# A two-layer encoder on one core: the second layer's SwiGLU of two prompt blocks in one loop, with gate and up as seven block products

## The chip, the core and the metric

One core of a Trainium2 chip runs the program. TensorE (PE) multiplies, VectorE (DVE), ScalarE (ACT) and GpSimd (POOL) do elementwise work, and DMA queues, issued here nearly always by SyncE (SP), move data between DRAM and on-chip memory. Each engine runs its own instructions in order and waits for the others by semaphores. The metric is the time of one execution in device microseconds (us). The kernel before takes 3156.17 us, the median of three runs (3152.59 to 3156.47).

## The reference

Two layers; the first mixes tokens with a Fourier transform, the second with attention; each is followed by a SwiGLU. Two sequences go through the same weights: a sample of 512 tokens and a prompt of 1024. Width is 1024, the hidden width of the SwiGLU is 2816.

```python
def swiglu_ffn(x, g, w_gate, w_up, w_down):
    h = rms_norm(x, g)
    return (jax.nn.silu(h @ w_gate) * (h @ w_up)) @ w_down

for i in range(DEPTH):
    j = i // 2
    if i % 2 == 0:
        x = x + fourier_mixer(x, norm_mix[i], fourier_w[j])
    else:
        x = x + attention_mixer(x, norm_mix[i], attn_w_qkv[j], attn_q_norm[j],
                                attn_k_norm[j], attn_w_o[j], cos, sin)
    x = x + swiglu_ffn(x, norm_ffn[i], w_gate[i], w_up[i], w_down[i])
```

## The kernel before, in words

Tokens are cut into three blocks of 512: block 0 is the sample, blocks 1 and 2 the prompt. Activations lie transposed, features on the 128 partitions and 512 tokens along them, so a block is 8 tiles of 128x512. Float32 matmuls are made of three: every operand is split into a rounded high half and the low rest (`split`, L219: a copy on ACT, L223, then a subtraction, L224, on POOL for weights and on DVE for the hidden chunk), and `mm3` (L229) multiplies high by high, high by low and low by high (L230 to L232). Its third matmul alone needs the low half of the weight.

`ffn(layer, b, ...)` (L636) is one SwiGLU of one block. It goes over 22 chunks of 128 hidden features. For each it loads three 128x1024 weights (gate, up, down; `weights`, L234, with buffers `raw` and `w`), makes gate and up into the two banks `g` with 24 matmuls each, then Silu on ACT (L675), the product on DVE (L676) and the split into `mid`. The chunk's eight down products (`down`: bank `c`, then an addition into `acc` on DVE, L650) are put on a list, `pend`, and drawn from it one by one between the matmuls of the next chunk.

While `ffn` runs as the main stream, a second stream prepares what comes later; `weave` (L814) mixes the two by paces given in estimated microseconds, and a scheduler then orders the instructions of each engine. The streams have buffers of their own, marked F (main) and X (second): four `w` buffers each, two `raw` each, in PSUM two `g` and two `c` banks for F, a pair of banks `a` and two `c` banks for X. In layer 1 the streams are: block 0's SwiGLU beside `aux_3` (the queries, keys and values of block 2, the attention of blocks 1 and 2, their output projections, `linear_residual` L621, which start from the attention output that `reloaded` L315 reads back from DRAM, and the norm of block 1); block 1's SwiGLU beside the norm of block 2; block 2's SwiGLU alone. The normed input h of a block, high and low, takes one of two buffers `h`. A norm starts with four small matmuls that spread the row factors (`in_rows`, L269), which need the sum of squares that the projection's last piece completes.

## Time and profile before

| what | before |
|---|---|
| median of three runs | 3156.17 us |
| the profiled execution: time, span | 3155.58 us, 3153.8 us |
| granted TensorE clock, mean | 0.989 |
| matmuls | 14646 |
| DMA traffic | 362.38 MB |

The profile gives busy times by engine, windows of the span, waits, and a timeline of single instructions. An entry such as `c<-mid,w` names what an instruction writes and what it reads. Matmuls are pipelined and their ends modelled, so their busy times overlap; the distance between starts is the time that one costs in a stream.

### The profile page before, as it was taken

How to read it: one execution, taken by the hardware profiler on the slowest of the kernel's cores; microseconds unless marked ns; L12 is line 12 of the kernel's file. 1: busy time of each engine (PE TensorE's matmuls, PEld its weight loads, DVE VectorE, ACT ScalarE, POOL GpSimd, SP SyncE). 2: the span in 40 equal slices, each digit the busy share in tenths (PEclk: the TensorE clock that was granted, in tenths of full speed). 3: DMA queues.
4: the chain of work that ended last, by engine and by line, in shares of the span. 5: the costliest groups of instructions: out<-in, count | busy, mean ns of one | idle time of the engine just before them, and what ended most of it. 6: DMA issues, size and time to landing. Idle time of an engine off the chain costs nothing.

```text
span 3153.8 us, 38178 instructions
## 1 busy us (share of the span) xinstructions
PE 3041.1 (96%) x14646; PEld 2523.0 (80%) x14646; DVE 1565.9 (50%) x2812; ACT 1253.2 (40%) x1806; POOL 1272.4 (40%) x583
## 2 busy tenths in 40 slices
PE   5699999999999999999999999999999999999999
PEld 4587788888877778888878788788788888888887
DVE  5664455453465643443464556666235445444444
ACT  5443332333266632333344477777323223222221
POOL 3444744434333454443433321312544444444443
PEclk9799999999999999999999999999999999999999
DMA  4424553333223544433343311212634333333332
GB/s 182 160 77 125 182 165 107 121 96 97 91 90 106 179 151 134 145 102 113 103 139 101 102 58 51 77 44 70 210 130 149 117 98 122 99 127 94 94 101 87
DMA packets 132091, 362.38 MB, mean 115 GB/s; under 512 B 15890, under 2 KB 24082, under 8 KB 131652
## 3 DMA queue, kind: packets, MB, share of 16 engines
q1 hardware_dynamic: 130468, 353.09, 35.3%
q10 hardware_dynamic: 1440, 6.85, 0.5%
q8 instruction: 115, 1.88, 0.2%
q14 instruction: 68, 0.56, 0.1%
HBM read 316.88 MB, written 43.00 MB: 114 GB/s over the span
## 4 chain that ended last, share of the span: by engine, by line
PE 84%; issue 4%; POOL 4%; DVE 3%; DMA 3%; ACT 2%; SPq 0%; POOLq 0%; ACTq 0%; DVEq 0%
PE g L230 14%; PE g L232 14%; PE g L231 14%; PE c L230 11%; PE c L231 11%; PE c L232 11%; POOL w L224 2%; PE c L787 2%; PE a L230 2%; PE a L232 2%; PE a L231 1%; DMA raw<-in_wf_dram 1%; DVE col L770 1%; PE c L720 1%; POOL raw L577 1%
## 5 line engine op out<-in xcount | busy, mean ns | idle before, releaser
L224 POOL TENSOR_TENSOR w<-raw,w 128x1024 fp32r<-128x1024 f32 (+1 forms) x496 | 1170.8, 2373 | 1760.7 <-ACT w L223 1749.9
L650 DVE TENSOR_TENSOR acc<-c,acc 128x512 f32<-128x512 f32 x1056 | 725.7, 689 | 788.1 <-PE c L232 784.1
L230 PE MATMUL g<-h,w 128*128 128x512 f32 x2112 | 830.2, 393 | 6.8 <-DVE h L227 6.5
L232 PE MATMUL g<-h,w 128*128 128x512 f32 x2112 | 826.3, 391 | 0.0
L231 PE MATMUL g<-h,w 128*128 128x512 f32 x2112 | 825.4, 391 | 0.0
L223 ACT CAST w<-raw 128x1024 fp32r<-128x1024 f32 (+1 forms) x496 | 513.8, 1038 | 744.2 <-PE c L232 533.0
L230 PEld LDWEIGHTS g<-h,w 128*128 128x128 f32 x2112 | 397.9, 188 | 86.8 <-DVE h L227 6.8
L232 PEld LDWEIGHTS g<-h,w 128*128 128x128 f32 x2112 | 397.6, 188 | 82.4 <-POOL w L224 0.3
L231 PEld LDWEIGHTS g<-h,w 128*128 128x128 f32 x2112 | 397.8, 188 | 78.9
L230 PE MATMUL c<-mid,w 128*128 128x512 f32 x1056 | 417.4, 396 | 12.2 <-DVE acc L650 9.6
L231 PE MATMUL c<-mid,w 128*128 128x512 f32 x1056 | 414.0, 392 | 0.6 <-DVE mid L224 0.6
L232 PE MATMUL c<-mid,w 128*128 128x512 f32 x1056 | 413.6, 392 | 0.0
L230 PEld LDWEIGHTS c<-mid,w 128*128 128x128 f32 x1056 | 198.7, 188 | 64.4 <-DVE acc L650 21.4
L675 ACT ACTIVATE t<-g 128x512 f32<-128x512 f32 x132 | 78.9, 597 | 404.4 <-PE g L232 404.0
L231 PEld LDWEIGHTS c<-mid,w 128*128 128x128 f32 x1056 | 199.1, 189 | 41.2 <-DVE mid L224 2.0
L232 PEld LDWEIGHTS c<-mid,w 128*128 128x128 f32 x1056 | 199.1, 189 | 41.1
L230 PE MATMUL c<-h,w 128*128 128x512 f32 x480 | 190.0, 396 | 1.4 <-ACT h L223 1.4
L231 PE MATMUL c<-h,w 128*128 128x512 f32 x480 | 188.4, 393 | 0.8 <-POOL h L224 0.8
L232 PE MATMUL c<-h,w 128*128 128x512 f32 x480 | 187.2, 391 | 0.0
L769 DVE TENSOR_REDUCE col<-a 128x1 f32<-128x1024 f32 (+1 forms) x96 | 100.3, 1045 | 127.0 <-PE a L232 126.8
L676 DVE TENSOR_TENSOR g<-g,t 128x512 f32<-128x512 f32 x132 | 92.0, 697 | 142.6 <-PE g L232 139.3
L224 DVE TENSOR_TENSOR mid<-g,mid 128x512 fp32r<-128x512 f32 x132 | 91.0, 690 | 88.1 <-ACT mid L223 87.7
(225 smaller groups left out, 3299.9 us busy)
## 6 DMA issues: line engine op xcount, KB each, us to landing
raw<-in_gate_dram SPq DMA_DIRECT2D x132, 512.0 KB, 3.5
raw<-in_up_dram SPq DMA_DIRECT2D x132, 512.0 KB, 3.6
raw<-in_down_dram SPq DMA_DIRECT2D x132, 512.0 KB, 3.6
t<-xres SPq DMA_DIRECT2D x80, 256.0 KB, 4.2
raw<-in_qkv_dram SPq DMA_DIRECT2D x36, 512.0 KB, 3.5
xres<-t SPq DMA_DIRECT2D x48, 256.0 KB, 3.0
acc<-xres SPq DMA_DIRECT2D x48, 256.0 KB, 4.7
raw<-in_wo_dram SPq DMA_DIRECT2D x24, 512.0 KB, 3.5
```

Of the source, the lines that this page charges most:

```text
L223: act.copy(hi, src)
L224: eng.tensor_tensor(lo, src, hi.bitcast(F32), op=ALU.subtract)
L230: pe.matmul(out, lh, rh, start=first, stop=False)
L231: pe.matmul(out, lh, rl, start=False, stop=False)
L232: pe.matmul(out, ll, rh, start=False, stop=last)
L577: pool.tensor_tensor(f[:, 1], raw[:, 0], raw[:, 1], op=ALU.subtract)
L650: dve.tensor_tensor(acc[dc], ps, acc[dc], op=ALU.add)
L675: act.activation(s, ga, AF.Silu)
L676: dve.tensor_tensor(up, up, s, op=ALU.mult)
L720: pe.matmul(c[:, i : i + 1], sq[:, i * P : (i + 1) * P], ones[:, 0:1], start=True, stop=True)
L769: dve.tensor_reduce(st[:, 0:1], s_in, op=ALU.max, axis=AX.X)
L787: pe.transpose(tr[:, i * P : (i + 1) * P], p[:, kc * P : (kc + 1) * P], ident)
```

## The change

The SwiGLU of blocks 1 and 2 in layer 1 becomes one loop, `ffn_pair`, over eleven pairs of chunks. For a pair, gate (and likewise up) is a product of a weight of 2 x 2 parts (two chunks, two halves of the 1024 features) with an activation of 2 x 2 parts (two halves of the features, two blocks). Instead of eight products of parts it makes seven, after Strassen and Winograd, of sums of parts. Each has one stationary weight operand (`operands`: four raw quarters a11, a12, a21, a22 and POOL's sums of them, each split as before) and one moving operand that is the same for all pairs: B11, B21, T2, T1, B22, T3 and N4, in this order. The results are added on DVE (`plus`) through the buffers U, V and W; with the second, fifth, sixth and seventh product a hidden chunk of one block is complete (`hidden`). Of the products two in three use a pair of banks held as one tile (`a`), every third the two `g` banks.

`moving` makes the seven moving operands from the normed blocks, by groups of four 128x512 pieces; five stay on chip, and T3 and N4 go through one buffer `l` to DRAM (`late`) and come back by a DMA that POOL issues (`moving_late`), into the buffer where block 0's h was. This stage and the first weights are the end of `aux_3`, which is now paced so that all of it ends within block 0's SwiGLU. The second stream's buffers are closed then, and the pair's take their place. The two `h` buffers are now told apart as A and B.

```diff
+    def open_pool(name, **kw):
+        opened[name] = tc.tile_pool(name=name, bufs=1, **kw)
+        pools[name] = opened[name].__enter__()
+        return pools[name]
...
-        "h": 2, "acc": 4, "mid": 2,
+        "hA": 1, "hB": 1, "acc": 4, "mid": 2,
         "wF": 4, "wX": 4, "rawF": 2, "rawX": 2, "tF": 3, "tX": 4, "ssF": 1, "ssX": 2, "pX": 2,
         "gF": 2, "gX": 1, "cF": 2, "cX": 2,
+        "mT": 5, "WT": 1, "tT": 6, "lT": 1, "rT": 4, "gT": 2,
...
+    def moving(blocks, gain, ops):
+        tp = open_pool("tT")
+        yield 2.0
+        r = [in_rows(rstd[b], lambda n: tl("t", [n], F32, "tT", tp)) for b in blocks]
+        yield 1.0
+        for j in range(4):
+            v = {}
+            for k in range(2):
+                for d in range(2):
+                    c = 4 * d + j
+                    x = tl("x", [TB], F32, "tT", tp)
...
+            a2 = bank2()
+            a, b = a2[:, 0], a2[:, 1]
...
+                dve.scalar_tensor_tensor(
+                    a if (d, k) == (0, 1) else x, x, gain[:, 4 * d + j : 4 * d + j + 1], r[k], op0=ALU.mult, op1=ALU.mult
+                )
+            def put(name, src, eng=None):
+                split(ops[name][:, 0, j], ops[name][:, 1, j], src, eng=eng)
+            def put_late(k, src):
+                x = tl("l", [2, TB], F32R, "lT", tp)
+                split(x[:, 0], x[:, 1], src, eng=pool)
+                sp.dma_start(late[:, k, :, j, :], x.bitcast(F32))
+            put("B11", v[0, 0], pool)
+            put("B21", v[1, 0], pool)
+            yield 6.0
+            dve.tensor_tensor(b, a, v[0, 0], op=ALU.subtract)
+            put("T1", b)
+            dve.tensor_tensor(v[0, 1], v[1, 1], a, op=ALU.subtract)
+            put_late(0, v[0, 1])
+            put("B22", v[1, 1], pool)
+            yield 6.0
+            dve.tensor_tensor(b, v[1, 1], b, op=ALU.subtract)
+            put("T2", b)
+            dve.tensor_tensor(v[0, 0], v[1, 0], b, op=ALU.subtract)
+            put_late(1, v[0, 0])
+            yield 6.0
+        close_pool("tT")
...
+    def moving_late(ops, k):
+        if k == 0:
+            m = h_slot("late", F32R, "A")[:, 0 : 16 * TB].rearrange("p (k h c n) -> p k h c n", k=2, h=2, c=4)
+            ops["T3"], ops["N4"] = m[:, 0], m[:, 1]
+        pool.dma_start(ops[("T3", "N4")[k]], late[:, k])
...
+        def some():
+            credit[0] += 0.62
+            while credit[0] >= 1.0:
+                credit[0] -= 1.0
+                if pend:
+                    pend.pop(0)()
...
+        def times(w, x):
+            turn[0] += 1
+            if turn[0] % 3 == 0:
+                banks = [bankg(), bankg()]
+            else:
+                g2 = tl("a", [2, TB], F32, "gT", gt)
+                banks = [g2[:, 0], g2[:, 1]]
+            for i in range(2):
+                for j in range(4):
+                    mm3(banks[i], w[:, 0, 4 * i + j], w[:, 1, 4 * i + j], x[:, 0, j], x[:, 1, j], j == 0, j == 3)
+                    some()
+                yield i, banks[i]
...
+        def operands():
+            for f0 in range(0, NF, 2):
+                a11, a12 = quarter(f0, 0), quarter(f0, 1)
+                yield stationary(a11)
+                a21, a22 = quarter(f0 + 1, 0), quarter(f0 + 1, 1)
+                yield stationary(a12)
+                s1 = raw_tile(2, TB)
+                pool.tensor_tensor(s1, a21, a22, op=ALU.add)
+                pool.tensor_tensor(a21, a11, a21, op=ALU.subtract)
+                pool.tensor_tensor(a11, s1, a11, op=ALU.subtract)
+                yield stationary(a11)
+                pool.tensor_tensor(a12, a12, a11, op=ALU.subtract)
+                yield stationary(s1)
+                yield stationary(a12)
+                yield stationary(a21)
+                yield stationary(a22)
...
+        def step(x):
+            w = ready.pop()
+            ready.append(next(ahead_))
+            yield from times(w, ops[x])
+        U, V, W = (tmp(), tmp()), (tmp(), tl("ss", [TB], F32, "ssF")), tl("W", [TB], F32, "WT", pools["mT"])
+        for f0 in range(0, NF, 2):
+            f1 = f0 + 1
+            for i, ps in step("B11"):
+                act.copy(U[i], ps)
+            if f0 == 0:
+                moving_late(ops, 0)
+                moving_late(ops, 1)
+            wd0 = weights(t["down"][layer, f0])
+            for i, ps in step("B21"):
+                plus(ps, ps, U[i])
+                if i == 0:
+                    s = silu(V[0], ps)
+                else:
+                    hidden(ps, s, f0, blocks[0], wd0)
+            for i, ps in step("T2"):
+                plus(U[i], ps, U[i])
+            for i, ps in step("T1"):
+                plus(V[i], ps, U[i])
+            for i, ps in step("B22"):
+                plus(ps, ps, V[i])
+                if i == 0:
+                    s = silu(W, ps)
+                else:
+                    hidden(ps, s, f0, blocks[1], wd0)
+            wd1 = weights(t["down"][layer, f1])
+            for i, ps in step("T3"):
+                plus(U[i], ps, U[i])
+                plus(ps, ps, V[i])
+                if i == 0:
+                    s = silu(V[0], ps)
+                else:
+                    hidden(ps, s, f1, blocks[1], wd1)
+            for i, ps in step("N4"):
+                plus(ps, ps, U[i])
+                if i == 0:
+                    s = silu(U[0], ps)
+                else:
+                    hidden(ps, s, f1, blocks[0], wd1)
...
+    def paced(stage, f):
+        for v in stage:
+            yield v * f
...
-        yield from qkv(2, kept[2])
-        yield from attend((1, 2))
+        yield from paced(qkv(2, kept[2]), 0.4)
+        yield from paced(attend((1, 2)), 0.65)
         for b in (1, 2):
-            yield from out_projection(b)
-        yield from prepare(1, 1)
-
-    def aux_4():
-        yield 100.0
-        yield from prepare(2, 1)
+            yield from paced(out_projection(b), 0.5)
+        close_pool("ap")
+        close_pool("sbX")
+        tp = open_pool("mT")
+        for name in ("B11", "B21", "T2", "T1", "B22"):
+            ops[name] = tl(name, [2, 4, TB], F32R, "mT", tp)
+        yield from moving((1, 2), g_ffn[1], ops)
+        close_pool("psX")
+        last["pair"] = ffn_pair(1, (1, 2), ops, t["y"])
+        cur[0] = "F"
+        v = next(last["pair"])
+        cur[0] = "X"
+        yield v
...
-    weave(ffn(1, 0, h_next, t["y"][0]), FFN_US, aux_3(), (QKV_US + 240.0 + 2 * LIN_US) * SLACK, 9)
-    weave(ffn(1, 1, h_next, t["y"][1]), FFN_US, aux_4(), 200.0)
-    weave(ffn(1, 2, h_next, t["y"][2]), FFN_US)
+    weave(ffn(1, 0, h_next, t["y"][0]), FFN_US, aux_3(), FFN_US, 9)
+    weave(last["pair"], 1.0)
```

Three places show how the order of instructions changes. First TensorE, where one chunk's last up matmul is followed by the next chunk, before (block 2; `h_21011` is its h):

```order
L231 MATMUL g_22794<-h_21011,w_22785 128x512
L232 MATMUL g_22794<-h_21011,w_22785 128x512
L230 MATMUL g_22904<-h_21011,w_22891 128x512
L231 MATMUL g_22904<-h_21011,w_22891 128x512
L232 MATMUL g_22904<-h_21011,w_22891 128x512
```

and in the changed loop, from the third place after the last matmul of B22's product (`late_19901` holds T3, here with weight `w_20923`, and N4, with `w_20973`; `mid_20965` is the hidden chunk that B22's product completed; in brackets the engines whose semaphores a row waits for):

```order
L244 MATMUL a_20976<-late_19901,w_20923 128x512
L245 MATMUL a_20976<-late_19901,w_20923 128x512
L246 MATMUL a_20976<-late_19901,w_20923 128x512
L244 MATMUL g_21044<-late_19901,w_20973 128x512 [waits Activation_49]
L245 MATMUL g_21044<-late_19901,w_20973 128x512
L244 MATMUL g_21045<-late_19901,w_20973 128x512
L245 MATMUL g_21045<-late_19901,w_20973 128x512
L246 MATMUL g_21044<-late_19901,w_20973 128x512 [waits Pool_49]
L244 MATMUL c_20983<-mid_20965,w_20744 128x512 [waits Activation_49]
```

Before, 18 matmuls of the next chunk's gate (three are shown) stand between the last up matmul and the first that reads `mid`. Now N4's first matmul stands six places after B22's last one, its first use of a low half ten, and the first reader of `mid` eleven.

Second POOL, which before made the low halves of three weights per chunk:

```order
L224 TENSOR_TENSOR w_23567<-raw_23565,w_23567 128x1024 [waits DMAHW5_49,Activation_49]
L224 TENSOR_TENSOR w_23668<-raw_23666,w_23668 128x1024 [waits DMAHW6_49,PE_49,Activation_49]
L224 TENSOR_TENSOR w_23673<-raw_23671,w_23673 128x1024 [waits DMAHW7_49,Activation_49]
L224 TENSOR_TENSOR w_23678<-raw_23676,w_23678 128x1024 [waits DMAHW0_49,Activation_49]
L224 TENSOR_TENSOR w_23779<-raw_23777,w_23779 128x1024 [waits DMAHW1_49,PE_49,Activation_49]
```

and now, from the low half of N4's weight in one pair to that of T2's in the next (`raw_22721`, `raw_22724`, `raw_22787` and `raw_22790` are the next pair's quarters a11 to a22, `raw_22853` their sum):

```order
L238 TENSOR_TENSOR w_22658<-raw_22369,w_22658 128x1024 [waits Activation_49]
L832 TENSOR_TENSOR raw_22853<-raw_22787,raw_22790 128x1024 [waits DMAHW2_49,DMAHW1_49,DMAHW3_49,DMAHW0_49,Pool_49]
L833 TENSOR_TENSOR raw_22787<-raw_22721,raw_22787 128x1024 [waits DMAHW4_49,Pool_49]
L238 TENSOR_TENSOR w_22727<-raw_22721,w_22727 128x1024 [waits Activation_49]
L834 TENSOR_TENSOR raw_22721<-raw_22853,raw_22721 128x1024 [waits Pool_49]
L238 TENSOR_TENSOR w_22793<-raw_22724,w_22793 128x1024 [waits DMAHW7_49,DMAHW6_49,Activation_49]
L836 TENSOR_TENSOR raw_22724<-raw_22724,raw_22721 128x1024 [waits Pool_49]
L238 TENSOR_TENSOR w_22850<-raw_22848,w_22850 128x1024 [waits DMAHW5_49,Activation_49]
L238 TENSOR_TENSOR w_22857<-raw_22721,w_22857 128x1024 [waits PE_49,Activation_49]
```

Between the weights stand four sums, and the first of them waits for the last quarter's load.

Third DVE, with the last chunks of layer 1's block with buffer `acc`; before, one chunk of block 1:

```order
L650 TENSOR_TENSOR acc_19688<-c_21733,acc_19688 128x512 [waits DVE_49,PE_49]
L650 TENSOR_TENSOR acc_19688<-c_21741,acc_19688 128x512 [waits DVE_49,PE_49]
L676 TENSOR_TENSOR g_21666<-g_21666,t_21755 128x512 [waits DVE_49,PE_49,Activation_49]
L224 TENSOR_TENSOR mid_21758<-g_21666,mid_21758 128x512 [waits Activation_49]
L650 TENSOR_TENSOR acc_19687<-c_21796,acc_19687 128x512 [waits DVE_49,PE_49]
L650 TENSOR_TENSOR acc_19687<-c_21804,acc_19687 128x512 [waits DVE_49,PE_49]
```

and now, under the fourth chunk from the end of block 0 (`x_19373` to `x_19377` are pieces of the second group of `moving`, `c_19182` and `c_19195` the row factors):

```order
L744 TENSOR_TENSOR x_19219<-x_19221,a_19227 128x512 [waits Pool_49]
L664 TENSOR_TENSOR acc_12867<-c_19349,acc_12867 128x512 [waits PE_49]
L664 TENSOR_TENSOR acc_12867<-c_19357,acc_12867 128x512 [waits PE_49]
L721 SCALAR_TENSOR_TENSOR x_19373<-x_19373,gains,c_19182 128x512 [waits DMAHW1_49]
L721 SCALAR_TENSOR_TENSOR a_19379<-x_19375,gains,c_19195 128x512 [waits DMAHW6_49,DVE_49]
L690 TENSOR_TENSOR g_19264<-g_19264,t_19388 128x512 [waits PE_49]
L721 SCALAR_TENSOR_TENSOR x_19377<-x_19377,gains,c_19195 128x512 [waits DMAHW7_49,Pool_49]
L238 TENSOR_TENSOR mid_19391<-g_19264,mid_19391 128x512 [waits Activation_49]
```

The chunk's product `g_19264` and its `mid_19391` now stand among the pieces of `moving`, behind one that waits for its load.

More of the change, by code (lines that the diff above doesn't have):

```diff
@@ L213, in trunk_kernel @@
     du = dram.tile([P, 2, 4, 514], F32, name="du")
+    late = dram.tile([P, 2, 2, 4, TB], F32, name="late")
     dot = [dram.tile([P, NC, TB], F32, name=f"dot{b}") for b in range(3)]
@@ L295, in new_residual, with normed @@
             rstd_cols(rstd[b], ss.pop(b), D)
-    def normed(b, gain, got, held=None):
+    def normed(b, gain, got, ab, held=None):
         yield 2.0
         r = in_rows(rstd[b])
-        h = h_tile()
+        h = h_tile(ab)
         yield 1.0
@@ L313, in normed, with reloaded @@
         got["h"] = h
[L315 to L317 removed]
+    def reloaded(d, got, ab):
+        h = h_tile(ab)
         for dc in range(NC):
@@ L344, in stats_rows @@
     def stats_rows(seq, n):
-        s = cp.tile([P, n], F32, name=f"s_{seq}")
-        r = cp.tile([P, n], F32, name=f"r_{seq}")
+        s = mpt.tile([P, n], F32, name=f"s_{seq}")
+        r = mpt.tile([P, n], F32, name=f"r_{seq}")
         xs = whole[seq]
@@ L355, in masked @@
     def masked(r, c):
-        m = cp.tile([P, 2], F32, name=nm("m"))
+        m = mpt.tile([P, 2], F32, name=nm("m"))
         dve.tensor_tensor(m[:, 0:1], r[:, c : c + 1], mask, op=ALU.mult)
@@ L681, in ffn @@
             one()
+    def moving(blocks, gain, ops):
[9 more added lines that the diff above has]
+                    x = tl("x", [TB], F32, "tT", tp)
+                    sp.dma_start(x, xres[blocks[k]][:, c, :])
+                    v[d, k] = x
+            a2 = bank2()
+            a, b = a2[:, 0], a2[:, 1]
+            for (d, k), x in v.items():
+                dve.scalar_tensor_tensor(
[22 more added lines that the diff above has]
+        close_pool("tT")
@@ new lines, in moving_late, with ffn_pair, down, quarter @@
+    def moving_late(ops, k):
[3 more added lines that the diff above has]
+        pool.dma_start(ops[("T3", "N4")[k]], late[:, k])
+    def ffn_pair(layer, blocks, ops, outs):
+        src = (t["gate"], t["up"])
+        raws, gt = open_pool("rT"), open_pool("gT", **PS)
+        accs = {}
+        for b in blocks:
+            halves = [acc_tile("acc", [4, TB], F32) for _ in range(2)]
+            accs[b] = [a[:, i] for a in halves for i in range(4)]
+        credit = [0.0]
+        def down(m, wd, fc, b, dc):
+            ps = bank()
+            mm3(ps, wd[:, 0, dc], wd[:, 1, dc], m[:, 0], m[:, 1], True, True)
+            acc = accs[b][dc]
+            if fc == 0:
+                sp.dma_start(acc, xres[b][:, dc, :])
+            dve.tensor_tensor(acc, ps, acc, op=ALU.add)
+            if fc == NF - 1:
+                new_residual(b, dc, acc, outs[b][:, dc, :])
+        def some():
[4 more added lines that the diff above has]
+                    pend.pop(0)()
+        def quarter(fc, half):
+            raw = tl("raw", [2, TB], F32, "rT", raws)
+            for i in range(2):
+                sp.dma_start(raw[:, i], src[i][layer, fc, :, half * TB : (half + 1) * TB])
+            return raw
+        def stationary(raw):
+            w = w_tile(2, NC, P)
+            flat = w.rearrange("p h c n -> p h (c n)")
+            split(flat[:, 0], flat[:, 1], raw.rearrange("p k n -> p (k n)"), eng=pool)
+            return w
+        turn = [0]
+        def times(w, x):
[5 more added lines that the diff above has]
+                banks = [g2[:, 0], g2[:, 1]]
+            for i in range(2):
+                for j in range(4):
+                    mm3(banks[i], w[:, 0, 4 * i + j], w[:, 1, 4 * i + j], x[:, 0, j], x[:, 1, j], j == 0, j == 3)
+                    some()
+                yield i, banks[i]
+        def hidden(up, s, fc, b, wd):
+            dve.tensor_tensor(up, up, s, op=ALU.mult)
+            m = tl("mid", [2, TB], F32R, "mid")
+            split(m[:, 0], m[:, 1], up)
+            pend.extend(lambda dc=dc: down(m, wd, fc, b, dc) for dc in range(NC))
+        def silu(s, x):
+            act.activation(s, x, AF.Silu)
+            return s
+        def plus(out, ps, x):
+            dve.tensor_tensor(out, ps, x, op=ALU.add)
+        def operands():
[14 more added lines that the diff above has]
+                yield stationary(a22)
+            yield None
+        ahead_ = operands()
+        ready = [next(ahead_)]
+        yield 15.0
+        def step(x):
[41 more added lines that the diff above has]
+                    hidden(ps, s, f1, blocks[0], wd1)
+            yield 1.0
+        while pend:
+            pend.pop(0)()
+        close_pool("gT")
+        close_pool("rT")
@@ L684, in qkv @@
     def qkv(b, held=None):
         got = {}
-        yield from normed(b, g_mix1, got, held)
+        yield from normed(b, g_mix1, got, "BAB"[b], held)
         h = got["h"]
@@ L886, in follow @@
         yield from mixer_projection("s", got_s, ahead)
-        yield from normed(0, g_ffn[0], first)
+        yield from normed(0, g_ffn[0], first, "B")
     def prepare(b, layer):
-        yield from normed(b, g_ffn[layer], nxt)
+        yield from normed(b, g_ffn[layer], nxt, "B" if b == 2 else "A")
     def h_next():
```

66 lines of the change are left out of this document (36 added, 30 removed).

## The prediction

> **What bounds the kernel now.** The page first: which engine is busy, and at what clock.
>
> ```profile
> span 3153.8 us, 38178 instructions
> PE 3041.1 (96%) x14646; PEld 2523.0 (80%) x14646; DVE 1565.9 (50%) x2812; ACT 1253.2 (40%) x1806; POOL 1272.4 (40%) x583
> ...
> PEclk9799999999999999999999999999999999999999
> ```
>
> TensorE (PE) is busy 96% of the span, at full clock after the start; no other engine passes 50%. The order of TensorE's instructions is the same in both programs up to one place: the last matmul of the second chunk of block 1's output projection. The timeline has that place, and windows from it to the end give the rest.
>
> ```profile
> 2229.29 0.39 PE L232 MATMUL c<-h,w 128*128 128x512 f32 x1
> 2229.52 0.39 PE L230 MATMUL g<-h,w 128*128 128x512 f32 x1
> ...
> 2229.50:2421.40 191.90, 191.38 (x853) 157.67 (x852) 80.52 (x145) 60.13 (x84) 83.02 (x40) 1.00 0.46 150
> 2421.40:2781.90 360.50, 360.30 (x1594) 298.23 (x1593) 162.50 (x236) 95.93 (x118) 157.64 (x67) 1.00 0.36 114
> 2781.90:3153.80 371.90, 366.19 (x1610) 301.26 (x1608) 159.09 (x230) 89.32 (x109) 154.54 (x65) 1.00 0.32 101
> ```
>
> The columns after the window are its length, then busy time and count of PE, weight load, VectorE (DVE), ScalarE (ACT) and GpSimd (POOL), then clock. The windows are the rest of layer 1's block 0, then block 1, then block 2. TensorE is full in all three, so what is saved must be matmuls, and what is lost will be waits that are not there today. TensorE's waits from 2400 on:
>
> ```profile
> PE c L230 <- ACT mid L223: 1.5, 1, 1.5
> PE c L230 <- DVE acc L650: 0.3, 1, 0.3
> PE c L231 <- DVE mid L224: 0.2, 1, 0.2
> ```
>
> Two microseconds in 754. The timeline at the end of one chunk of block 2 prices everything that follows:
>
> ```profile
> 2716.52 0.39 PE L232 MATMUL g<-h,w 128*128 128x512 f32 x1
> ...
> 2716.03 4.76 POOL L224 TENSOR_TENSOR w<-raw,w 128x1024 fp32r<-128x1024 f32 x2 [4.60 <-ACT w L223]
> 2716.99 1.06 ACT L223 CAST w<-raw 128x1024 fp32r<-128x1024 f32 x1 [1.03 <-PE g L232]
> 2717.00 0.70 DVE L676 TENSOR_TENSOR g<-g,t 128x512 f32<-128x512 f32 x1 [1.41 <-PE g L232]
> 2717.95 0.58 ACT L223 CAST mid<-g 128x512 fp32r<-128x512 f32 x1
> 2718.46 0.33 SPq L237 DMA_DIRECT2D raw<-in_gate_dram  x1
> 2718.55 0.69 DVE L224 TENSOR_TENSOR mid<-g,mid 128x512 fp32r<-128x512 f32 x1 [0.85 <-ACT mid L223]
> 2720.60 0.39 PE L232 MATMUL g<-h,w 128*128 128x512 f32 x1
> 2720.82 0.39 PE L230 MATMUL c<-mid,w 128*128 128x512 f32 x1
> ```
>
> A matmul lasts 0.39 here, but from 2716.52 to 2720.60 there are 18 steps: 4.08 / 18 = 0.2267 us each. They overlap, and **0.2267 is the price of a matmul**, not 0.39. Others: an engine that waits for a matmul starts 0.47 after its start (2716.99); the hidden chunk has its high half 2.0 us (2718.53) and its low half 2.7 us (2719.24) after the last up matmul. The 18 matmuls put ahead of the first down product, 4.1 us, hide that.
>
> **What is removed.** Today two chunks for two blocks take 4 x 48 = 192 gate and up matmuls; the seven products take 7 x 24 = 168. Over 11 pairs of chunks 264 go: 264 x 0.2267 = **59.8 us**. The down products and the norms' matmuls stay in number. By the mean duration in the groups (393 ns) one would get 104 us, which is wrong, since these matmuls overlap. [...]
>
> **What is added** is work for the other engines, and less distance between producer and consumer.
>
> ```profile
> L224 POOL TENSOR_TENSOR w<-raw,w 128x1024 fp32r<-128x1024 f32 x484 | 1155.6, 2400 | 1739.5 <-ACT w L223 1728.7 <-PE c L232 5.3 <-PE a L232 5.2
> L224 POOL TENSOR_TENSOR h<-t,h 128x512 fp32r<-128x512 f32 x24 | 30.4, 1295 | 7.3 <-ACT h L223 7.3
> L223 ACT CAST w<-raw 128x1024 fp32r<-128x1024 f32 x484 | 506.5, 1048 | 736.7 <-PE c L232 533.0 <-PE g L232 86.9 <-POOL raw L577 47.3
> L650 DVE TENSOR_TENSOR acc<-c,acc 128x512 f32<-128x512 f32 x1056 | 725.7, 689 | 788.1 <-PE c L232 784.1
> L227 DVE SCALAR_TENSOR_TENSOR h<-a,gains,h 128x512 fp32r<-128x512 f32 x64 | 47.8, 748 | 13.2 <-ACT h L226 13.1
> raw<-in_gate_dram SPq DMA_DIRECT2D x132, 512.0 KB, 3.5
> t<-xres SPq DMA_DIRECT2D x80, 256.0 KB, 4.2
> raw<-dqk SPq DMA_DIRECT2D x30, 256.0 KB, 2.7
> ```
>
> A pair is 168 + 96 = 264 matmuls, 59.8 us. In it POOL has 9 low halves of weights and 4 sums of 128x1024, 13 x 2.40 = 31.2 us; DVE has 14 product sums, 8 for the hidden chunks and 32 down additions, 54 x 0.69 = 37.3 us; ACT has 9 x 1.05 + 10 x 0.6 = 15.5 us. **Loads fit; latencies decide.** The sums' price is that of the row of 128x1024, the nearest one.
>
> *Pair loop, weights.* The four weight buffers hold two down chunks, the operand in use and the next one. N4's operand takes the buffer that B22 leaves: 0.47 + 1.05 + 0.08 + 2.40 = 4.0 us after B22's last matmul its low half is there, or 18 matmuls. In the order N4 needs it 10 matmuls after in three of eleven pairs (21 or more in the others): 3 x 8 x 0.2267 = 5.4. Only then is the fourth quarter's raw buffer free: its load (3.4 with the issue, between the 2.7 and 3.5 of the rows), two sums and the low half of the next B11, 3 x 2.40, follow on POOL, 4.0 + 3.4 + 7.3 = 14.7 us or 65 matmuls after B22. The order has B11 at 59, 64, 74, 77, 64, 74, 56, 64, 74 and 59: short by 24 matmuls in all, 5.4.
> *Pair loop, banks.* 52 of the 77 products put gate and up into one tile of two banks, and there the up half waits until the gate half is read. Behind the waiting matmul stands all of TensorE's queue. With a sum alone the reader needs 0.47 + 0.69 + 0.05 = 1.2 us, and the order leaves 4 matmuls between, 1.1 us with the step itself; with Silu too 1.8 against 1.8 (7 matmuls). That is at most 0.1 each, 3 in all, and 36 if a down addition (0.69) always stands ahead on DVE. For the loop I take 5.4 + 5.4 + 3 less what overlaps, **13**; ends 0 and 36.
>
> *The moving operands* are made under the last four chunks of block 0: 288 matmuls, 65.3 us, stand on TensorE behind the norms' rows. In them DVE has 16 x 0.75 + 24 x 0.69 of this stage and 40 x 0.69 of the chunks, 56 us, and POOL 20 x 1.295 + 12 x 2.40, 55 us. Six x buffers serve groups of four, so in groups 2 to 4 a load (4.2) that waits for a buffer stands on DVE ahead of a chunk's g<-g,t, which has 4.1 - 2.7 = 1.4 us to spare: up to 3 x 2.8. I take **6**; ends 0 and 17 (all four groups late by a load).
> *The first pair.* From its start POOL has one weight, two DMA issues, a down weight, four sums and T2's weight, 7 x 2.40 and what is still ahead of them, one more, 19.2 us. T2 wants its low half some 77 matmuls after the start, 17.5 us. A DMA issue from POOL isn't in the trace; SP's is 0.33 us, two make 0.7. I take **3**; ends 0 and 8. [...]
> *Output projections* stand closer together: 60 matmuls lie between the two where 72 did, 2.7 us less cover for reading the attention output back (8 x 1.295 on POOL). I take **2**; ends 0 and 6.
> *End.* Some 15 down products remain after the last N4 in place of 8, and the timeline shows two of them per 1.75 us in place of 1.36:
>
> ```profile
> 3145.72 0.40 PE L230 MATMUL c<-mid,w 128*128 128x512 f32 x1
> ...
> 3147.47 0.40 PE L230 MATMUL c<-mid,w 128*128 128x512 f32 x1
> ```
>
> That is 7 x 0.2 = 1.4 more, and the older ones hide the 1.5 us wait for mid shown above: nothing in all.
> *At nothing:* the two norms of block 1 and 2 (they move from later blocks, where 0.5 us of waits stood), the reload of T3 and N4 through DRAM (needed 156 matmuls, 35 us, after its buffer is free; 2 MB is four times the 3.5 us row), and half the gate and up traffic. Without that cover the reload would cost 14 us once.
>
> **Sum.** 59.8 - 13 - 6 - 3 - 2 = 35.8. The profiled execution took 3155.6 (span 3153.8 and 1.8 around it), the median of the runs is 3156.2: 3155.6 - 35.8 = **3119.8, forecast 3120**.
>
> **Rivals.**
> 1. *TensorE never waits.* All of 59.8 comes: 3096. For it: block 1 and 2 show 0.5 us of waits today, and POOL and DVE are loaded by half. Against it: the order leaves 10 matmuls where 18 are needed. With the terms at half: up to 3108.
> 2. *DVE's or POOL's queue binds in the loop.* The loop's end of 36 in place of 13: 3143; with some of the other ends, up to 3150. For it: 54 DVE instructions per pair in bursts; DVE can be in a down addition when a product ends. Against: DVE is idle 38% of a pair.
> 3. *Slower: weights come late at every product.* A product takes 59.8 / 7 = 8.5 us, and its successor's weight can start only when its predecessor leaves a buffer. With POOL free that takes 4.0 us. Each POOL instruction ahead adds 2.40: with two it is 8.8, with three 11.2. All of the gain is eaten at 59.8 / 77 = 0.8 us per product, so from a little over two ahead at every product. At two and a half ahead, 10.0 - 8.5 = 1.5 x 77 = 116: 3212. Against it: POOL is busy 31 of 60 us, and the order places most operands' first use 30 matmuls or more after the buffer is left.
> 4. *The second stream doesn't end within the first block.* Then TensorE stands at B11. The order has 288 matmuls there; only if the stage took over 125 us would all be lost. Between, some 50 us late: 3165 at the worst; within 0.2% at 30 to 40.
>
> **Chances.** Forecast (3108 to 3132) 0.52; rival 1 0.22; rival 2 0.16; rival 3 0.05; rival 4 0.05. The range leaves out what lies below 3096 (0.03), the far end of rival 2 and the two last: 3096 to 3146. About 0.2% (3150 to 3162) is what a measurement of this kernel can tell from no change. Faster: 0.52 + 0.22 + 0.16 = 0.90; same 0.03 and slower 0.02 of rival 4; with rival 3 slower is 0.07.
>
> **What would show it.** TensorE's count falls by 264 to 14382. In the loop a pair takes 60 to 62 us; waits of PE on POOL's w stand at N4 and at the next B11, and on DVE and ACT at the up halves. Ahead of the loop, DVE waits for x loads, and PE for mid, in the last three chunks of block 0. Wrong would be: pairs of 59.8 (rival 1), of 63 or more (rival 2) or of 68 with POOL without a gap (rival 3), or a PE gap of 10 us before the first product (rival 4).

## The result, and the profile after

The changed kernel takes 3131.7 us, the median of four runs (3126.0 to 3136.2); the kernel before took 3156.2 in the same comparison. The ratio is 0.9924, with a 95% interval of 0.9905 to 0.9943: **24 us faster**, where 36 were forecast (3120, range 3096 to 3146).

The page of after, its lines on the span and the engines:

```profile
span 3134.4 us, 37508 instructions
PE 3005.0 (96%) x14382; PEld 2471.0 (79%) x14382; DVE 1656.4 (53%) x2974; ACT 1243.9 (40%) x1807; POOL 1325.6 (42%) x616
...
PEclk9799999999999999999999999999999999999999
```

TensorE has 264 matmuls less and the same share of busy time. Now windows of after, from the place where TensorE's order begins to differ: attention's rest and output projections, the stage of the moving operands, and from the first product to the end (length, then busy time and count by engine, clock, DMA share, GB/s):

```profile
2233.40:2360.70 127.30, 127.00 (x574) 104.72 (x573) 43.29 (x89) 38.47 (x56) 55.57 (x28) 1.00 0.50 164
2360.70:2434.70 74.00, 68.75 (x290) 54.82 (x289) 51.34 (x80) 31.06 (x47) 49.87 (x32) 0.98 0.58 193
2434.70:3134.40 699.70, 682.89 (x2929) 543.58 (x2927) 399.86 (x604) 166.06 (x209) 342.54 (x145) 1.00 0.20 66
```

They add to 901.0; before, the same work took 191.9 + 360.5 + 371.9 = 924.3. So 23.3 us are gained here. The place itself comes 3.9 us later than before (2233.4 against 2229.5), with the same instructions ahead of it; in the later profiles it comes anywhere from 2224.8 to 2233.4, so this is spread and not the change.

For 2927 steps of 0.2267 the last window would need 663.6 us, and 4.4 go by after the last matmul's start: 31.7 us are stops, that is, time by which the distance of two starts exceeds a step. TensorE's waits in that window name a part of them (engine, line, what it waits for; total, times, longest):

```profile
PE a L246 <- POOL w L238: 6.2, 4, 1.8
PE g L246 <- POOL w L238: 5.1, 6, 1.3
PE c L244 <- DVE acc L771: 0.6, 3, 0.2
PE a L244 <- ACT t L818: 0.2, 1, 0.2
```

L244 to L246 are `mm3` in the changed kernel, L237 and L238 `split`, L771 the pair's down additions, L818 Silu, L822 the additions of products. The third matmul of a weight, which alone needs its low half, waits for POOL. The timeline of the third pair has such a wait at N4's weight:

```profile
2604.76 1.05 ACT L237 CAST w<-raw 128x1024 fp32r<-128x1024 f32 x1 [3.14 <-PE a L246]
...
2605.89 2.38 POOL L238 TENSOR_TENSOR w<-raw,w 128x1024 fp32r<-128x1024 f32 x1 [6.79 <-ACT w L237]
...
2606.66 0.40 PE L245 MATMUL g<-late,w 128*128 128x512 f32 x1
...
2608.29 0.33 SPq L786 DMA_DIRECT2D raw<-in_gate_dram  x1
...
2608.32 0.50 PE L246 MATMUL g<-late,w 128*128 128x512 f32 x1 [1.26 <-POOL w L238]
```

ACT had to wait for B22's last matmul to leave the buffer; the low half was ready at 2608.27, and TensorE, after a last start at 2606.66, went on at 2608.32: 1.43 us more than a step. Only then (2608.29) is the next quarter's load issued.

The view of waits misses the short stops. They can be seen between the starts of neighbouring matmuls, here where B21's up half waits for its tile of two banks (timeline of after):

```profile
2635.32 0.70 DVE L822 TENSOR_TENSOR a<-a,t 128x512 f32<-128x512 f32 x1 [0.74 <-PE a L246]
...
2636.06 0.60 ACT L818 ACTIVATE t<-a 128x512 f32<-128x512 f32 x1 [3.35 <-DVE a L822]
...
2636.41 0.39 PE L244 MATMUL g<-T,w 128*128 128x512 f32 x1
2636.71 0.50 PE L244 MATMUL a<-B,w 128*128 128x512 f32 x1
2637.05 0.40 PE L245 MATMUL a<-B,w 128*128 128x512 f32 x1
2637.28 0.39 PE L246 MATMUL a<-B,w 128*128 128x512 f32 x1
```

The sum and Silu read the gate half until 2636.66. The up half's first matmul starts at 2636.71, 0.30 after its neighbour: a wait of 0.07. But the matmul behind it comes 0.34 later, 0.11 more than a step, and only the next is at 0.23 again. **This stop of 0.07 costs 0.18.**

If each step's excess over 0.2267 is put down to the matmul that waits at its end (the order lists which do), and the excess of the next step to the same stop, each step counted once, the last window divides like this:

| TensorE's stop, from the first product on | stops | waited, us | next steps, us |
|---|---|---|---|
| low half of a product's weight (POOL) | 11 of 77 | 13.1 | 1.1 |
| up half, until its tile's gate half is read (ACT, DVE) | 37 of 52 | 1.6 | 4.0 |
| down product (mid, or its bank `c`; the end too) | 26 | 3.5 | 2.8 |
| first matmul of a product (ACT) | 3 | 0.6 | 0.3 |
| eight steps at half clock (last section) behind one of the late low halves | | | 1.7 |
| steps too long by less than 0.06 | | | 3.0 |

That is 31.7 in all.

### The profile page after: what moved, and what is told of

It is laid out like the page before. It is cut to its first block, busy times and chain, and to the rows that moved or that the text cites. A ratio compares the mean times of both kernels' runs of the same rounds, so it can differ in the third digit from the quotient of the medians.

```text
span 3134.4 us, 37508 instructions
## 1 busy us (share of the span) xinstructions
PE 3005.0 (96%) x14382; PEld 2471.0 (79%) x14382; DVE 1656.4 (53%) x2974; ACT 1243.9 (40%) x1807; POOL 1325.6 (42%) x616
## 5 line engine op out<-in xcount | busy, mean ns | idle before, releaser
L238 POOL TENSOR_TENSOR w<-raw,w 128x1024 fp32r<-128x1024 f32 (+1 forms) x463 | 1093.4, 2371 | 1632.9 <-ACT w L237 1596.3
L237 ACT CAST w<-raw 128x1024 fp32r<-128x1024 f32 (+1 forms) x463 | 479.2, 1038 | 754.8 <-PE c L246 357.2
L244 PE MATMUL g<-h,w 128*128 128x512 f32 x1408 | 557.2, 396 | 6.8 <-DVE h L241 6.5
L246 PE MATMUL g<-h,w 128*128 128x512 f32 x1408 | 553.7, 394 | 0.0
L245 PE MATMUL g<-h,w 128*128 128x512 f32 x1408 | 552.9, 393 | 0.0
L244 PE MATMUL c<-mid,w 128*128 128x512 f32 x1056 | 419.9, 399 | 17.3 <-DVE acc L664 15.2
L246 PE MATMUL c<-mid,w 128*128 128x512 f32 x1056 | 413.9, 392 | 0.0
L771 DVE TENSOR_TENSOR acc<-c,acc 128x512 f32<-128x512 f32 x352 | 240.9, 689 | 192.8 <-PE c L246 192.0
L244 PEld LDWEIGHTS g<-h,w 128*128 128x128 f32 x1408 | 266.1, 189 | 59.7 <-DVE h L241 6.8
L246 PEld LDWEIGHTS g<-h,w 128*128 128x128 f32 x1408 | 266.0, 189 | 55.1 <-POOL w L238 0.3
L245 PEld LDWEIGHTS g<-h,w 128*128 128x128 f32 x1408 | 266.2, 189 | 52.1
L244 PEld LDWEIGHTS c<-mid,w 128*128 128x128 f32 x1056 | 198.6, 189 | 80.1 <-DVE acc L664 27.4
L246 PEld LDWEIGHTS c<-mid,w 128*128 128x128 f32 x1056 | 199.0, 188 | 41.5
L244 PE MATMUL c<-h,w 128*128 128x512 f32 x480 | 189.9, 396 | 1.7 <-ACT h L237 1.7
L246 PE MATMUL c<-h,w 128*128 128x512 f32 x480 | 187.2, 391 | 0.0
L987 ACT ACTIVATE p<-a,col,rqc 128x1024 f32<-128x1024 f32 (+1 forms) x96 | 102.3, 1066 | 65.7 <-DVE col L984 65.3
L689 ACT ACTIVATE t<-g 128x512 f32<-128x512 f32 x88 | 52.6, 598 | 175.4 <-PE g L246 175.1
```

The source lines that it names most:

```text
L237: act.copy(hi, src)
L238: eng.tensor_tensor(lo, src, hi.bitcast(F32), op=ALU.subtract)
L244: pe.matmul(out, lh, rh, start=first, stop=False)
L245: pe.matmul(out, lh, rl, start=False, stop=False)
L246: pe.matmul(out, ll, rh, start=False, stop=last)
L689: act.activation(s, ga, AF.Silu)
```

## Experiments

Each kernel was timed in five rounds beside the kernel before. "Moving" is the window of the moving operands' stage in its profile, "rest" the one from the first product to the end.

| kernel | median, us | ratio to before, interval | moving | rest |
|---|---|---|---|---|
| again (unchanged) | 3133.8 | 0.9927 [0.9913, 0.9940] | 72.7 | 699.0 |
| down_late | 3118.5 | 0.9880 [0.9866, 0.9893] | 74.0 | 686.6 |
| late_stores_pool | 3137.0 | 0.9937 [0.9924, 0.9949] | 79.8 | 697.7 |
| price | 3186.5 | 1.0093 [1.0080, 1.0107] | 73.9 | 754.6 |
| single_banks | 3114.2 | 0.9864 [0.9849, 0.9879] | 72.2 | 677.6 |
| eight_x | 3131.0 | 0.9910 [0.9897, 0.9924] | 74.3 | 697.1 |
| two_l | 3129.3 | 0.9907 [0.9894, 0.9920] | 73.8 | 694.9 |
| down_late_banks | 3111.0 | 0.9849 [0.9835, 0.9862] | 74.7 | 677.4 |
| banks_again | 3109.9 | 0.9853 [0.9839, 0.9867] | 72.0 | 678.7 |
| banks_lag | 3107.3 | 0.9848 [0.9834, 0.9862] | 74.2 | 676.2 |
| banks_x_act | 3112.8 | 0.9862 [0.9847, 0.9876] | 72.8 | 679.8 |
| banks_price | 3168.6 | 1.0042 [1.0028, 1.0056] | 72.9 | 736.6 |

### The unchanged kernel

> The changed kernel once more, as the reference for the others of this group: 3131.7 us, give or take 3. It also tells two readings of the first profile apart. There TensorE reached the place from which its order changes at 2233.4 us, before the change 2229.5, though up to that place it does the same. If that is spread between executions, the place lies somewhere between 2229 and 2234 this time. If it belongs to the change, it lies at 2233 again. In both readings N4's weight is late by 1.4 us in pairs 3, 6 and 9, since the order fixes that.

The place lies at 2226.6 here, below even the 2229 to 2234 that spread was expected to give. N4's waits stand in pairs 3, 6 and 9 with 1.43 us each, as in the first profile.

### When a weight's buffer comes free

```diff
-            wd1 = weights(t["down"][layer, f1])
             for i, ps in step("T3"):
+                if i == 0:
+                    wd1 = weights(t["down"][layer, f1])
```

> The second down weight of a pair is asked for after N4's operand instead of before it, so N4's operand takes a buffer that is free already and no longer the one that B22 leaves. Theory (a buffer comes free late, and through N4's raw quarter that delays the next pair's load, sums and B11): N4's three waits of 1.43 go (4.3 us), B11's of 2.0, 0.9, 1.7, 0.4 and 1.4 go (6.4 us), and so does the half-rate stretch of 1.9 us behind the first of them: about 12.6 us less than the unchanged kernel, some 3119. Rival, POOL's queue as such is too long: it does as much as before, so the waits only change places, and the time stays within 2 us. Third, the down weight now comes late instead: TensorE waits at the first down product after T3, 3 us or more per pair, and the time grows by 20 or more.

It is 15.3 us faster than the unchanged kernel, and the rest falls by 12.4 (699.0 to 686.6). TensorE's waits there:

```profile
PE a L246 <- POOL w L238: 1.7, 1, 1.7
PE c L244 <- DVE acc L771: 0.4, 2, 0.2
PE g L246 <- POOL w L238: 0.3, 1, 0.3
PE a L244 <- ACT t L818: 0.2, 1, 0.2
```

From the second pair on no low half is late; only two of the first pair stay, those of the first product and of T2. POOL does the same work, so its queue as such was not the cause: **the buffer that N4's operand waited for was**, and through it the next pair's quarter, sums and B11. The short stops stay (table after the next group).

### What a matmul costs here

In B21, T2 and T1 a fourth matmul, low half by low half, is added to each `mm3`:

```diff
+                    if more:
+                        pe.matmul(banks[i], w[:, 1, 4 * i + j], x[:, 1, j], start=False, stop=j == 3)
```

> Adds the product of the low halves (a fourth matmul to each three) in B21, T2 and T1: 24 matmuls per pair, 264 in all, as many as the change removed, so that TensorE has 14646 again. Theory (a matmul costs its step, 0.2267 us, and waits stand elsewhere, at N4, the next B11 and the moving operands): 59.8 us more than the unchanged kernel, about 3191, and N4's waits unchanged. Rival, price by the duration of 0.39: 103 us more, about 3235. Third, the loop is bound by POOL's or DVE's work so that TensorE has time left: under 50 us more.

52.7 us more in the median, and 55.6 in the rest. The stops in the rest fell from 31.1 to 26.8 us (again to price), since the new matmuls cover some. Growth and lost stops add up to 264 steps by the way of counting, since a stop is what exceeds a step. What can be tried is whether the growth nears 59.8 where little is left to cover; that is done below.

### One tile of two banks, or single banks

```diff
-                g2 = tl("a", [2, TB], F32, "gT", gt)
-                banks = [g2[:, 0], g2[:, 1]]
+                banks = [tl("a", [TB], F32, "gT", gt) for _ in range(2)]
...
-        ... "gT": 2,
+        ... "gT": 4,
```

> The two pairs of banks that hold gate and up as one tile become four single banks, so that the up half no longer waits until the gate half is read. Theory (each such wait is short, but costs twice: the wait itself, and a longer step of the matmul behind it): in the profiles so far 40 of 52 up halves stop TensorE, 1.7 to 2.0 us of waits and 4.0 to 4.3 us in the steps behind them. Both go: 5 to 6 us less than the unchanged kernel, some 3128, and the rows of an up half 0.11 us long behind a stop disappear. Rival, the wait alone counts: 2 us less. Third, DVE's additions are what is late, and the wait moves to the next product's first matmul: within 1 us.

It is about 20 us faster than the unchanged kernel (0.63% by the ratios), over three times what was expected, and the rest falls by 21.4. Its window, then TensorE's waits in it:

```profile
2427.70:3105.30 677.60, 670.17 (x2929) 546.98 (x2928) 404.32 (x604) 166.43 (x209) 342.73 (x145) 1.00 0.20 68
```

```profile
PE a L246 <- POOL w L238: 1.7, 1, 1.7
PE g L246 <- POOL w L238: 0.8, 1, 0.8
PE c L244 <- DVE acc L771: 0.4, 2, 0.2
```

Not only the up halves' stops are gone, the late low halves behind the first pair are too, although buffers and POOL's work are as before. TensorE's order tells why. In the changed kernel, third pair (a row each: number, line, output, operands; `late_19901` is T3, `B_3265_19162` is B22):

```
11171 L246 a_20926<-B_3265_19162,w_20867
11172 L244 a_20976<-late_19901,w_20923
...
11178 L244 a_20976<-late_19901,w_20923
11179 L244 a_20926<-B_3265_19162,w_20867
...
11190 L246 a_20926<-B_3265_19162,w_20867
...
11196 L244 g_21044<-late_19901,w_20973
...
11211 L244 a_20976<-late_19901,w_20923
```

Since the up half of B22 must wait for its gate half, the scheduler has put seven matmuls of T3 ahead of it, and B22's weight is left those seven later. T3's up half (from 11211) must wait in the same way, and there N4 (weight `w_20973`) has gone ahead. So only five of T3's 24 matmuls lie between B22's last and N4's first; with single banks all 24 do. Of 76 neighbouring products 30 overlap like this; with single banks it is one:

| matmuls from the last use of B22's weight | with pairs of banks | with single banks |
|---|---|---|
| to N4's low half | 10, 10, 10, 21 (four times), 35 or 38 | 42 (39 at the end) |
| to the next B11's low half | 56 to 77 | 81 |

So there are two ways to end the late weights, an earlier buffer or an order without overlap, and **the second removes their cause**.

> Both edits of the loop together, the late down weight and the single banks. Theory: they act at different waits, so the loop is shorter by their sum: 12.5 + 5 to 6, some 18 us less than the unchanged kernel, 3114 to 3116. Rival, what is taken away at one place comes back at the next: less than 15 us.

The rest is 677.4, against 677.6 with single banks alone: the late down weight adds nothing. The two edits act at the same wait and not at different ones; that the gain still passed the expected sum of 18 is due to the single banks alone.

The stops of the rest, in the four profiles (us waited and, after the plus, in the next steps):

| stop | unchanged | down_late | single_banks | banks_lag |
|---|---|---|---|---|
| low halves | 13.1 + 1.1 | 2.3 + 0.2 | 2.9 + 0.2 | 2.8 + 0.2 |
| up halves | 1.6 + 4.0 | 1.6 + 4.5 | 0 | 0 |
| down products | 3.5 + 2.8 | 3.8 + 3.05 | 3.3 + 2.0 | 2.55 + 2.1 |
| first matmuls | 0.6 + 0.3 | 0 | 0 | 0 |
| half clock, small excesses | 1.7 + 3.0 | 0 + 3.1 | 0 + 1.3 | 0 + 0.6 |
| in all | 31.7 | 18.6 | 9.7 | 8.3 |

### The moving operands

The stage has 288 matmuls, 65.3 us of steps, and takes 72 to 74.7 in all kernels but late_stores_pool. The timeline of after shows how DVE and TensorE lose time there (the x load in question was issued at 2384.66):

```profile
2384.66 0.43 SPq L716 DMA_DIRECT2D x<-xres  x1
...
2388.04 0.37 SPq L731 DMA_DIRECT2D late<-l  x1
...
2388.53 0.75 DVE L721 SCALAR_TENSOR_TENSOR x<-x,gains,c 128x512 f32<-128x512 f32 x1 [2.23 <-DMA x<-xres]
2389.19 0.68 DVE L664 TENSOR_TENSOR acc<-c,acc 128x512 f32<-128x512 f32 x1
...
2389.93 0.50 PE L244 MATMUL c<-mid,w 128*128 128x512 f32 x1 [1.75 <-DVE acc L664]
```

DVE's scaling of a piece waits 2.23 us for its load; the down addition stands behind it, holds its bank `c`, and TensorE's next down product waits 1.75 us. Three edits each took one suspect away.

```diff
-                sp.dma_start(late[:, k, :, j, :], x.bitcast(F32))
+                pool.dma_start(late[:, k, :, j, :], x.bitcast(F32))
```

> The eight stores of T3's and N4's pieces to DRAM are issued by POOL, right behind the subtraction that they wait for, and no longer by SP. Theory (loads of x stand on SP behind those stores, DVE waits for x, and down additions wait behind it on DVE): SP's waits of 16 us for POOL there go, DVE's waits for x fall from 9.8 us to under half, and the stage of the moving operands takes 69 to 71 us instead of 74.0: 3 to 5 us less than the unchanged kernel. Rival, the six x buffers set the loads' start: within 1 us of the unchanged kernel, with the same waits of DVE for x. Third, issuing costs POOL so much that the weights' low halves come late: up to 3 us more.

```diff
-                    x = tl("x", [TB], F32, "tT", tp)
+                    x = tl("x", [TB], F32, "tT", tp) if k == 0 else tl("x", [TB], F32, "ssF") if d else tl("x", [TB], F32, "WT", pools["mT"])
```

> Two buffers that lie idle until the pair loop (V's second and W) hold two pieces of each group of four, so that the moving operands have eight x buffers in place of six. Theory (loads of x wait for a buffer, DVE waits for the load, down additions wait behind it): DVE's waits for x fall from 9.8 us to under 5, the waits of TensorE for DVE's additions of 1.9 and 2.7 us shrink, and the stage takes 70 to 72 us in place of 73 to 74: 2 to 4 us less. Rival, the one buffer l holds ACT and with it everything: within 1 us.

The second l has that edit and, in addition, the new sizes:

```diff
-        ... "tT": 6, "lT": 1, ...
+        ... "tT": 4, "lT": 2, ...
```

> The same two idle buffers, but the room that they free goes to a second buffer l, so that there are six x buffers as before. Theory for this one (ACT waits 10 us in 3 waits for l's store and the casts of mid and of x behind it are late): ACT's waits for the store go, and the stage takes 70 to 72 us: 2 to 4 us less than the unchanged kernel. Rival, the x buffers decide: within 1 us. If this and the run with eight x buffers both gain, both queues share the price.

None of them gains in this stage: 79.8, 74.3 and 73.8 us. With eight x buffers DVE still waits 8.9 us for x, with the second `l` 9.1 (9.8 in after), although ACT's waits for the store, 10.3 us in after, are gone there. With the stores on POOL, TensorE's waits of that stage are now two large ones:

```profile
PE c L244 <- DVE acc L664: 4.2, 1, 4.2
PE c L244 <- ACT mid L237: 3.9, 2, 3.5
```

The second is new. ACT's waits in the same stage of that kernel:

```profile
ACT l L237 <- DMA late<-l: 25.6, 6, 6.8
```

In after these were 10.3 us in 3. The stores now leave POOL in its own order, and the one buffer `l` holds ACT, whose cast of `mid` stands behind. Whether SP held the stage this run can't tell: DVE's waits for x didn't fall (11.8 us), and SP now stood 13.9 us at the loads of x until POOL had read their buffers. The median of two_l (4.5 us below the unchanged kernel) comes with no shorter stage, and its interval and that of again overlap.

A gain of a microsecond or two can't be read from this stage's length: in again, single_banks and banks_again (72.0 to 72.7) TensorE is at full clock throughout it. In the other profiles it also has stretches at half clock (last section): three in late_stores_pool, two in eight_x, one in each of the rest.

### What is left on top of the single banks

> The kernel with four single banks once more, as the reference of this group. It took 19.6 us less than the unchanged kernel where 5 to 6 were expected. The order of TensorE's instructions explains it: with pairs of banks 30 of 76 neighbouring products overlap (the next product's matmuls stand ahead of the waiting up half), so B22's weight is left late and N4's low half is wanted 10 matmuls later in three pairs; with single banks one neighbour pair overlaps, N4 is wanted 39 to 42 and the next B11 81 matmuls later. If that holds, the loop takes 673 us again, with no wait for a low half after the first pair, and the time is 3109 to 3116.

As expected: 3109.9, a rest of 678.7, and no late low half after the first pair.

```diff
+            tick[0] += 1
...
+                if pend and due.get(pend[0], 0) > tick[0]:
+                    break
...
+            due.update({f: tick[0] + 6 for f in new})
```

> On top of the single banks, a hidden chunk's down products are not drawn until six groups of three gate and up matmuls have been issued after it, so that 19 or more matmuls stand ahead of the first one in place of 11. Theory (what is left of the loop's waits, some 7 us, is down products that come too early for mid): the waits at the first down product go, about 12 of 0.1 us with steps of 0.1 us behind them, 2 to 3 us less than the reference of this group. Rival, the stops of the last eight down products are most of it, and the delay adds one or two products there: no gain, or 1 us more.

The rest falls by 2.5 us (678.7 to 676.2; 1.4 against the first run of the single banks), and twelve of the thirteen stops at a first down product that waits for ACT are gone, all but the one at the end. The medians, 2.5 us apart as well, can't be told apart by their intervals.

> On top of the single banks, eight x buffers as before, and the loads of x are issued by ACT and no longer by SP. Theory (SP works its DMAs off in order, and the loads of x stand behind weight loads that wait for a buffer, 30 us of waits in this stage, and behind the late stores, 16 to 21 us): DVE's waits for x fall below 4 us, and the stage of the moving operands takes 68 to 71 us in place of 72 to 75: 2 to 6 us less than the reference. Rival, ACT now waits for the x buffers itself and the casts behind them are late: the stage is as long as before or longer.

The edit is that of eight_x with `act.dma_start` for the loads, on top of the single banks. DVE's waits in the stage, in this kernel:

```profile
DVE T L238 <- ACT T L237: 8.5, 4, 4.3
...
DVE a L721 <- DMA x<-xres: 2.5, 3, 1.8
```

and in after:

```profile
DVE a L721 <- DMA x<-xres: 7.6, 3, 3.9
...
DVE x L721 <- DMA x<-xres: 2.2, 1, 2.2
DVE T L238 <- ACT T L237: 0.7, 1, 0.7
```

The waits for x fell from 9.8 to 2.5 us as the theory said (banks_again has 9.4), and the stage did not get shorter (72.8 against 72.0): DVE now waits for ACT's cast of T, and ACT in turn for POOL:

```profile
ACT T L237 <- POOL l L238: 10.7, 3, 5.1
```

The wait has in the main changed its name.

> On top of the single banks, the 264 matmuls with the two low halves again. With pairs of banks they cost 52.7 us, and the loop alone grew by 55.6, since its waits fell from 31.1 to 26.8 us. Theory (a matmul costs its step, and the rest was waits that the additional matmuls covered): here there is hardly a wait to cover, so the loop grows by 59 to 60 us. Rival, a matmul costs less in this place than its step elsewhere: the loop grows by 53 to 56 again.

The windows of the rest, of banks_again and of this kernel:

```profile
2427.10:3105.80 678.70, 670.75 (x2930) 546.71 (x2928) 404.27 (x604) 166.39 (x209) 342.72 (x145) 1.00 0.21 68
2430.30:3166.90 736.60, 729.95 (x3193) 596.32 (x3192) 404.94 (x604) 166.57 (x209) 342.91 (x145) 1.00 0.19 62
```

The rest grows by 57.9 us, the median by 58.8. That is just under the 59 to 60 expected and above the rival's 53 to 56. Stops fell from 10.6 to 8.8 us; half of that is one stop of 0.9 at T2's low half, which the longer B21 ahead of it now covers. So in this place **a matmul costs its step but for what it covers**.

## Why the prediction was right, and where its sizes were off

The direction, the bound and the range held; the time came 11.7 us above the forecast. The stops are set against what stood in the same places before (2.25 us in the projections, 0.6 in the rest of block 0, 4.25 after it, by the same count):

| term | predicted | measured, net of before |
|---|---|---|
| 264 matmuls | -59.8 | -59.8 |
| output projections | 2 | 0.6 |
| moving operands | 6 | 8.1 (1.6 of it half clock) |
| pair loop, first pair and end | 13 + 3 + 0 | 27.5 |
| sum | -35.8 | -23.6 (windows: -23.3) |

The first line is the count times the step; banks_price, which puts as many matmuls back, gave 57.9. Of the 12.2 us that are missing in the sum, 11.5 are the loop's.

**The price of a matmul.** Right. 0.2267 is the step, not the duration of 0.39: the two price runs, 55.6 and 57.9 us in the rest, exclude the 103 us that the duration gives. The median distance of two starts is 227 ns in after too, from the first product to the end.

**Weights.** Right in place and size: N4 in three pairs cost 3 x 1.43 = 4.3 us (5.4 predicted; the order quoted ahead of the prediction is that of pair 3). The six late B11 cost 2.0 + 0.9 + 0.1 + 1.7 + 0.4 + 1.4 = 6.5 (5.4 predicted), in just the six pairs in which the order leaves under 65 matmuls. down_late showed the mechanism. What the prediction did not see is that the distances of 10 and 56 in the order, which it took as given, come from the tile of two banks: it listed *weights* and *banks* as two terms, and single_banks showed one cause.

**Banks.** The step that failed in size: "at most 0.1 each, 3 in all". 37 of 52 up halves stop, and they cost 5.6, because the step behind each stop is longer by some 0.11. The waits alone, 1.6, would have been within the term. Nor is 5.6 what the tile of two banks costs: by the order that it brings about, the single banks saved 21.4 us in the rest.

**Down products, first matmuls and slow steps.** The terms that were missing. The loop's sum had nothing for stops at down products and first matmuls; they cost 7.2 us together, 2.8 of them after the last N4. The end itself was put at nothing, rightly: 3.0 us are lost after the last N4, where 3.4 stood before (1.6 for `mid`, which older down products now hide, and 1.8 for the banks `c`). That leaves 4.4 within the loop. The half clock's 1.7 and the 3.0 of slightly longer steps were not in the sum either. The order quoted ahead of the prediction shows the first reader of `mid` eleven places behind the end of a product, and N4's first matmul six behind B22; the prediction compared only the weights' distances with latencies. banks_lag, which puts 19 or more matmuls ahead, removes twelve of these stops; those at the end stay.

**First pair.** 3 predicted. The low half of the first product's own weight was late by 1.8, T2's by 0.5: right in size, but mostly at another weight than the one worked out. The two DMA issues took POOL 1.2 us, where 0.7 stood in the sum. The reload of T3 and N4 was hidden: its two loads landed 8.1 and 14.2 us after their issue, where 14 were estimated.

**Moving operands.** 8.1 for 6, and 6.8 in the second profile (again), which has no half clock there. The cause named, loads of x on which DVE waits ahead of the chunks' work, is in the trace, but the victim was the down addition and its bank more than the chunk's product: TensorE waits 5.0 us for `acc` in this stage and 0.2 for `mid`. And it is not the only limit: with the waits for x gone the stage stayed as it was. Which edit would shorten it is open; eight x buffers (also with their loads issued by ACT), a second `l` and stores by POOL were tried, but not all together.

**Rivals.** TensorE never waiting (3096) fell: nine low halves were late behind the first pair, as counted from the order. DVE's or POOL's queue binding came half true by its sign: from one end of N4 to the next, pairs 2 to 11 took 60.0 to 63.8 us, 61.8 in the mean, so some reached its mark of 63, but with single banks the same work on DVE and POOL ran with 10 us of stops in the whole rest, so no queue was bound. Weights late at every product, and a second stream that doesn't end in time, did not occur: there is no gap ahead of the first product beyond its 1.8.

## What to carry to other kernels

Two results in one tile couple their release: whoever needs the second waits for the reader of the first (37 of 52 up halves stopped here), and a scheduler that works around this wait can hold another buffer longer, so that the visible wait (here POOL's low halves, 13.1 us) stands far from its cause. Where one engine is full, count for every producer the matmuls that stand between it and its consumer, and price a tie as a stop, since even a stop of 0.07 us cost 0.18 here by the longer step behind it. And an edit that removes the wait named by the profile may only rename it (here DVE's waits for x fell from 9.4 to 2.5 us, and the stage took 72.8 us after 72.0): look at the stage's length, not at the wait.

## What the hardware showed that was not expected

- After most stops, even some of 0.04 us, the next step is longer: 0.34 in place of 0.23 us (rows at 2636.71 and 2637.05; the stopped matmul shows 0.50 in place of 0.39). In the unchanged loop these steps cost 8.2 us, against 13.1 for the waits for late low halves.
- After some stops TensorE ran at half clock, in before behind one of 1.6 us (up to 2215.11; mean clock 0.51 from 2217.00 to 2220.38). Windows of after around a stop of 2.75 us in the stage of the moving operands (the column behind POOL is the clock):

```profile
2402.00:2408.50 6.50, 6.50 (x29) 5.07 (x27) 3.20 (x5) 1.53 (x2) 6.16 (x4) 1.00 0.70 215
2408.50:2411.20 2.70, 0.11 (x2) 0.07 (x1) 1.47 (x3) 0.62 (x1) 1.27 (x2) 1.00 0.93 292
2411.90:2415.30 3.40, 3.40 (x9) 2.65 (x8) 2.89 (x5) 1.07 (x2) 1.28 (x1) 0.50 0.41 157
2415.30:2420.00 4.70, 4.70 (x22) 3.83 (x21) 3.48 (x7) 3.52 (x5) 2.40 (x2) 1.00 0.02 3
```

  For 3.4 us the steps are 0.427, which costs 1.6 us more, and it sets in 0.8 us after work has resumed. The length of the one stop doesn't decide. In after, one of 2.0 at the second pair's B11 did the same, and one of 1.8 at the first product did not. In the other profile of this kernel (again) it is the other way round: after one of 2.7 in the stage of the moving operands the clock stays full, after one of 1.9 at the first product it is halved (both windows of again):

```profile
2404.80:2408.20 3.40, 3.40 (x15) 2.82 (x16) 3.33 (x6) 1.21 (x2) 1.29 (x1) 1.00 0.54 207
2430.30:2433.60 3.30, 3.30 (x10) 2.56 (x8) 0.83 (x2) 0.00 (x0) 3.28 (x4) 0.50 0.35 91
```

  In after, from 2200 us on, half clock sets in at 2220.77, 2411.92 and 2493.84 and lasts 3.4 us each time. What decides whether a stop is followed by it is not shown: no run here was made to find that out.
